# Six instead of four pairs of k's of a down projection as seven products for eight, on one core

## The chip, the cores and the metric

The kernel runs on one core of one Trainium2 chip. The metric is the device time of one execution in microseconds (us): the median of the runs before is 2079.3 us, over three runs from 2079.28 to 2080.11. All matrix work is done in pieces of float32: each operand is split into a high part (`hi`, rounded to the type `float32r`) and the rest (`lo`), and a product is three matmuls: hi x hi, hi x lo and lo x hi.

## The reference

The reference is a block of two layers on an activation `h` of 256 rows and 2048 columns. The first layer mixes with an S5 scan and a gated recurrence, the second with sliding-window attention. After each there is the same feed-forward part, and the change lies in its last product:

```python
def squared_relu_mlp(xn, w_up, w_down):
    return jnp.square(jax.nn.relu(xn @ w_up)) @ w_down

h = h + y.astype(h.dtype)
h = h + squared_relu_mlp(rms_norm(h, mlp_norm[layer]), mlp_w_up[layer], mlp_w_down[layer]).astype(h.dtype)
```

`w_up` is 2048 x 8192 and `w_down` 8192 x 2048, in float32. Every weight is read from HBM once or, in the mixed products below, partly twice.

## The kernel before

**Units.** All weights come in units of 512 KB (128 partitions x 1024 float32), in one list that is written out ahead of the program (`units`). For each unit there is a DMA on the queue of SP (`emit_dma`, line 108 for the units of sums, line 113 for plain ones), a copy on ScalarE (ACT) to the high part (line 141) and a subtraction on VectorE (DVE) to the low part (line 142). `advance` hands the next unit's halves to TensorE (PE) and issues as many DMAs and splits ahead as the buffers allow. Raw units have four buffers of their own (`raw`); while a feed-forward part runs, every odd unit lies instead in one of four "home" buffers in a scratch tile, which the trace calls `chi`. The split halves have four buffers (`whi`, `wlo`) and, for every second odd unit, two more in a scratch tile that the trace calls `clo`.

**The feed-forward part.** The 8192 inner columns are worked off in four chunks of 2048. `up(c)` computes a chunk in eight blocks of 256 columns (32 units); at the end of each block DVE and ACT square, scale and split the result into `ch[c]`. `down(c)` adds the chunk's product with `w_down` to `h`. For the last chunk this is a plain product; for the first three chunks of each layer, six in all, it is `down_mixed`.

**The mixed down projection.** The chunk has 16 k's (blocks of 128 rows of `w_down`), taken as eight pairs. For the columns 0 to 1023 (n = 0 and 1) a pair of k's, the two halves of the 256 rows and the two column halves form a 2 x 2 by 2 x 2 block product. That takes eight products plainly (24 matmuls of 512 columns); the first `NS` = 4 pairs take seven (21 matmuls), from sums of the activations (`forms`, computed at the end of blocks 0 to `NS` - 1 of `up`, lines 1025 to 1032) and from sums of weights (`combine`, line 120 on DVE). A pair's weights come as four units of kinds of their own: "t1" and "t42" in a first half of the stage, "b2" and "b12" (half a unit) in a second. t42 is combined with the raw t1, which has to stay until then, and b12 with the raw b2. On PE a t1, t42 or b2 is 6 matmuls, a b12 3, and a plain unit 12. The columns n = 2 and 3 are plain (16 units) and are strewn between the others; the pairs from `NS` on of n = 0 and 1 are plain units at the end.

**What sets the order.** `down_plan` is the order of the units on PE. The program is scheduled as a whole when it is built, so the order on each engine can differ a little from the order in the code. DVE, ACT and SP work their instructions off in the order that stands there. Scratch tiles such as the block results `r`, the sums `s_` and the copies in `down_mixed` come from one pool of six 4 KB buffers (`t4`).

Of the kernel before, what the change touches and what calls it, by code (L numbers as in the profile page):

```python
# [9 lines left out]
F32R = mybir.dt.float32r  # L10
# [7 lines left out]
P = 128  # L18
# [42 lines left out]
def hybrid_kernel(ctx: ExitStack, tc: tile.TileContext, x, even_norm, even_w_in, s5_lambda_re, s5_lambda_im,  # L61
# [10 lines left out]
    sp = ctx.enter_context(tc.tile_pool(name="sp", bufs=6))  # L72
# [105 lines left out]
    def pump(budget):  # L178
        while side and budget > 0:
            try:  # L180
                budget -= next(side[0])
            except StopIteration:
                side.pop(0)

    def drain(g=None):
        while side and (g is None or g in side):
            pump(1.0)

    def mm(o, a, b, start, stop, **kw):
        PE.matmul(o, a, b, start=start, stop=stop, skip_group_check=True, **kw)  # L190
# [18 lines left out]
    def ublock(XT, kts):  # L209

        acc = psA.tile([P, 2, 2, T], F32, tag="acc", name="acc")
        n = len(kts)
        for i in range(0, n, 4):
            hi, lo = advance()
            for kk in range(4):
                k = kts[i + kk]
                for m in range(2):
                    mm(acc[:, m], hi[:, kk, m * P:(m + 1) * P], XT.both[:, :, k, :], i + kk == 0, False)
                for m in range(2):
                    mm(acc[:, m, 0], lo[:, kk, m * P:(m + 1) * P], XT.hi[:, k, :], False, i + kk == n - 1)  # L220
            pump(SIDE)
        return acc
# [26 lines left out]
    def pm(shape, dtype=F32):  # L249
        return psM.tile(shape, dtype, tag="m", name="m")  # L250

    def t4(shape, dtype=F32):
        return sp.tile(shape, dtype, tag="t4", name="t4")

    def new_pair(kind, shape=(P, KD, T)):
        if kind == "x":
            b = bp.tile([P, 2] + list(shape[1:]), F32R, tag="x", name="x", bufs=1)
            pair = Pair(b[:, 0], b[:, 1])
            pair.both = b
            return pair  # L260
        bufs = 2
        return Pair(bp.tile(list(shape), F32R, tag=kind + "hi", name=kind + "hi", bufs=bufs),
                    bp.tile(list(shape), F32R, tag=kind + "lo", name=kind + "lo", bufs=bufs))
# [43 lines left out]
        ends.append(len(units))  # L307


    NS = 4  # L310
    plain = [(None, n, i) for n in (2, 3) for i in range(8)]
    down_plan = []
    for j in range(NS):
        down_plan += [("t1", 0, j), plain.pop(0), ("t42", 0, j), plain.pop(0)]
        if j < 2:
            down_plan.append(plain.pop(0))
    for j in range(NS):
        down_plan += [("b2", 0, j), plain.pop(0), ("b12", 0, j)]
        if plain and j < 2:
            down_plan.append(plain.pop(0))  # L320
    down_plan += plain + [(None, n, i) for n in (0, 1) for i in range(NS, 8)]

    add_mlp(0)
# [563 lines left out]
    for i in range(10):  # L887
# [14 lines left out]
        hh, j = divmod(i - 2, 4)  # L902
# [81 lines left out]
    def mlp(norm, nxt):  # L984
        XT = norm.XT
        ch, forms = {}, {}
# [20 lines left out]
        def up(c):  # L1007
            ch[c] = new_pair("c")
            if c < 3:
                forms[c] = sp.tile([P, 2, NS, 4, P], F32R, tag="q1", name="forms", bufs=1)  # L1010
            for n in range(8):
                acc = ublock(XT, K16)
                drain()
                r = t4([P, 2, T])
                S.copy(out=r, in_=acc[:, :, 1])
                V.tensor_tensor(out=r, in0=acc[:, :, 0], in1=r, op=ALU.add)
                V.scalar_tensor_tensor(out=r, in0=r, scalar=0.0, in1=rst.unsqueeze(1).to_broadcast([P, 2, T]),
                                       op0=ALU.max, op1=ALU.mult)
                S.activation(out=r, in_=r, func=AF.Square)
                ks = slice(2 * n, 2 * n + 2)  # L1020
                S.copy(out=ch[c].hi[:, ks, :], in_=r)
                V.tensor_tensor(out=ch[c].lo[:, ks, :], in0=r, in1=ch[c].hi[:, ks, :].bitcast(F32),
                                op=ALU.subtract)
                if c < 3 and n < NS:
                    a11, a21, a12, a22 = [r[:, k, t * P:(t + 1) * P] for k in range(2) for t in range(2)]
                    s_ = t4([P, 4, P])
                    for o, a, b, op in ((0, a21, a22, ALU.add), (1, a11, s_[:, 0], ALU.subtract),
                                        (2, a11, a21, ALU.subtract), (3, a12, s_[:, 1], ALU.add)):
                        V.tensor_tensor(out=s_[:, o], in0=a, in1=b, op=op)
                    fh, fl = forms[c][:, 0, n], forms[c][:, 1, n]  # L1030
                    S.copy(out=fh, in_=s_)
                    V.tensor_tensor(out=fl, in0=s_, in1=fh.bitcast(F32), op=ALU.subtract)

        def hadd(t, n, o):
            cs = slice(n * 512, (n + 1) * 512)
            V.tensor_tensor(out=h[:, t, cs], in0=o, in1=h[:, t, cs], op=ALU.add)  # L1036

        def down_mixed(c):
            X, F = ch[c], forms[c]
            a_, c_, e_, f_ = [pm([P, 512]) for _ in range(4)]  # L1040
            half = {0: (a_, f_), 1: (c_, e_)}
            s15, s6v = t4([P, 2, 512]), t4([P, 2, 512])
            s1, s5, s6, v = s15[:, 0], s15[:, 1], s6v[:, 0], s6v[:, 1]
            accs = {}

            def triple(o, fh, fl, wh, wl, start, stop):
                mm(o, fh, wh, start, False)
                mm(o, fh, wl, False, False)
                mm(o, fl, wh, False, stop)

            def whole(k, t):
                return X.hi[:, k, t * P:(t + 1) * P], X.lo[:, k, t * P:(t + 1) * P]

            def form(j, i):
                return F[:, 0, j, i], F[:, 1, j, i]

            for kind, n, j in down_plan:
                hi, lo = advance()
                w = [(hi[:, b], lo[:, b]) for b in range(2)]
                if kind == "t1":  # L1060
                    triple(a_, *whole(2 * j, 0), *w[0], j == 0, False)
                    triple(c_, *form(j, 0), *w[1], j == 0, False)
                elif kind == "t42":
                    triple(f_, *whole(2 * j + 1, 1), *w[0], j == 0, False)
                    triple(e_, *form(j, 1), *w[1], j == 0, False)
                    if j == NS - 1:
                        S.copy(out=s1, in_=a_)
                        S.copy(out=s5, in_=c_)
                        S.copy(out=s6, in_=e_)
                elif kind == "b2":  # L1070
                    triple(a_, *whole(2 * j + 1, 0), *w[0], False, False)
                    triple(c_, *form(j, 3), *w[1], False, False)
                elif kind == "b12":
                    triple(e_, *form(j, 2), *w[0], False, j == NS - 1)
                    if j == NS - 1:
                        V.tensor_tensor(out=v, in0=e_, in1=s1, op=ALU.add)
                        hadd(0, 1, s1)
                        hadd(0, 1, s6)
                        hadd(1, 0, v)
                        hadd(1, 1, v)  # L1080
                        hadd(1, 1, s5)
                else:
                    if n not in accs:
                        if n > 1:
                            acc = psA.tile([P, 2, 512], F32, tag="acc", name="acc")
                            accs[n] = [acc[:, t] for t in range(2)]
                        else:
                            accs[n] = half[n]
                    for t in range(2):
                        for kk in range(2):  # L1090
                            first = j + kk == 0 if n > 1 else n == 1 and t == 1 and j == NS and kk == 0
                            triple(accs[n][t], *whole(2 * j + kk, t), *w[kk], first, j == 7 and kk == 1)
                    if j == 7:
                        for t in range(2):
                            hadd(t, n, accs[n][t])
                    pump(SIDE)
# [12 lines left out]
        for c in range(4):  # L1109
            up(c)  # L1110
            down(c)
# [205 lines left out]
```

## Time and profile before

| | |
|---|---|
| median of the runs | 2079.3 us |
| the profiled execution | 2076.72 us |
| its span, first to last instruction | 2074.9 us |
| PE busy | 2062.2 us |
| DVE busy | 1476.6 us |
| ACT busy | 1137.5 us |
| granted TensorE clock | 1.000 over the span |

"Busy" counts the time in which an engine works on at least one instruction. The durations of matmuls overlap (a matmul of 512 columns is listed with about 390 ns), so the time of one in a stream is read from the distance of two starts. The first mixed down projection lies from 510.73 to 596.39 us.

### The profile page before, as it was taken

To read this page: it belongs to the slowest core of one execution; us is meant where nothing else is said; L and a number is where in the kernel's file an instruction comes from. 1 tells how busy PE (TensorE), PEld (TensorE's weight loads), DVE (VectorE), ACT (ScalarE), POOL (GpSimd) and SP (SyncE) were. 2 spreads that over 40 slices of the span, in tenths; PEclk is the share of its full clock that TensorE was granted. 3 is DMA by queue.
4 is the path that set the end of the run, shared out by engine and by line. 5 is a ranking of instruction groups with operands and counts; after the bars stand their busy time and mean duration, and the time that the engine had idled before them with its cause. 6 is when DMAs were issued, how large, how long until landed. Compare 5 with 4: busy or idle time off the path is not lost. (4 is left out here: it accounts for less than half of the span.)

```text
span 2074.9 us, 31132 instructions
## 1 busy us (share of the span) xinstructions
PE 2062.2 (99%) x12144; PEld 1755.4 (85%) x12144; DVE 1476.6 (71%) x2100; ACT 1137.5 (55%) x1541; POOL 38.8 (2%) x38
## 2 busy tenths in 40 slices
PE   9999999999999999999999999999999999999999
PEld 8988988888888878888888888788888888888887
DVE  6799967777767767776655688777767776776653
ACT  5887554565545545554554477565545545554542
POOL 2000000000000000000000110000000000000000
PEclk9999999999999999999999999999999999999999
DMA  8444557565676586576554643556676576567552
GB/s 250 122 150 145 169 165 245 173 199 193 204 244 191 192 254 190 196 250 197 192 184 125 190 150 125 183 182 203 204 249 188 192 260 192 187 210 247 188 200 89
DMA packets 264739, 397.75 MB, mean 192 GB/s; under 512 B 14888, under 2 KB 148560, under 8 KB 264272
## 3 DMA queue, kind: packets, MB, share of 16 engines
q1 hardware_dynamic: 263168, 392.50, 59.7%
q8 instruction: 95, 1.56, 0.3%
q0 software_dynamic: 672, 2.15, 0.3%
q10 hardware_dynamic: 752, 1.12, 0.2%
q14 instruction: 52, 0.43, 0.1%
HBM read 393.62 MB, written 2.10 MB: 191 GB/s over the span
## 5 line engine op out<-in xcount | busy, mean ns | idle before, releaser
L141 ACT CAST whi<-raw 128x1024 fp32r<-128x1024 f32 (+1 forms) x479 | 494.1, 1034 | 524.8 <-PE acc L190 427.5
L142 DVE TENSOR_TENSOR wlo<-raw,whi 128x1024 fp32r<-128x1024 f32 (+1 forms) x479 | 571.0, 1200 | 243.5 <-ACT whi L141 242.7
L190 PE MATMUL acc<-x,whi 128*128 128x512 f32 (+1 forms) x2336 | 636.0, 359 | 0.0
L190 PEld LDWEIGHTS acc<-x,wlo 128*128 128x128 f32 x1952 | 367.7, 189 | 70.2 <-DVE wlo L142 0.3
L190 PE MATMUL acc<-x,wlo 128*128 128x256 f32 x1952 | 417.9, 279 | 0.1
L190 PEld LDWEIGHTS acc<-x,whi 128*128 128x128 f32 x2336 | 359.6, 190 | 1.5 <-issue 0.4
L190 PE MATMUL acc<-wlo,chi 128*128 128x512 f32 x664 | 260.1, 392 | 2.6 <-DVE wlo L142 2.4
L190 PE MATMUL acc<-whi,chi 128*128 128x512 f32 x664 | 260.4, 392 | 0.0
L190 PE MATMUL acc<-whi,clo 128*128 128x512 f32 x664 | 259.4, 391 | 0.0
L142 DVE TENSOR_TENSOR wlo<-chi,whi 128x1024 fp32r<-128x1024 f32 x138 | 165.5, 1199 | 108.4 <-ACT whi L141 108.3
L141 ACT CAST whi<-chi 128x1024 fp32r<-128x1024 f32 x138 | 142.5, 1032 | 160.7 <-PE acc L190 123.7
L141 ACT CAST clo<-chi 128x1024 fp32r<-128x1024 f32 x136 | 143.0, 1053 | 137.6 <-PE acc L190 110.0
L142 DVE TENSOR_TENSOR clo<-chi,clo 128x1024 fp32r<-128x1024 f32 x136 | 166.1, 1223 | 58.1 <-ACT clo L141 57.0
L190 PE MATMUL acc<-whi,x 128*128 128x512 f32 x576 | 181.4, 393 | 0.0
L190 PE MATMUL acc<-x,clo 128*128 128x512 f32 x960 | 176.9, 337 | 0.0
L190 PEld LDWEIGHTS acc<-x,clo 128*128 128x128 f32 x960 | 150.2, 188 | 21.3
L190 PEld LDWEIGHTS acc<-wlo,chi 128*128 128x128 f32 x664 | 124.7, 188 | 31.7 <-DVE wlo L142 6.8
L190 PEld LDWEIGHTS acc<-whi,chi 128*128 128x128 f32 x664 | 124.7, 188 | 26.4 <-issue 0.8
L190 PEld LDWEIGHTS acc<-whi,clo 128*128 128x128 f32 x664 | 124.7, 188 | 25.3
L190 PEld LDWEIGHTS acc<-whi,x 128*128 128x128 f32 x576 | 107.4, 188 | 22.4 <-issue 0.4
L190 PE MATMUL acc<-clo,chi 128*128 128x512 f32 x400 | 123.1, 389 | 0.0
L120 DVE TENSOR_TENSOR raw<-raw 128x512 f32<-128x512 f32 (+1 forms) x72 | 59.4, 824 | 89.0 <-DMA raw<-in_mlp_w_down_dram 52.7
(260 smaller groups left out, 2399.6 us busy)
## 6 DMA issues: line engine op xcount, KB each, us to landing
chi<-in_mlp_w_down_dram SPq DMA_DIRECT2D x146, 512.0 KB, 3.8
raw<-in_mlp_w_up_dram SPq DMA_DIRECT2D x134, 512.0 KB, 3.8
raw<-in_mlp_w_down_dram SPq DMA_DIRECT2D x134, 512.0 KB, 4.6
chi<-in_mlp_w_up_dram SPq DMA_DIRECT2D x122, 512.0 KB, 3.8
raw<-in_even_w_in_dram SPq DMA_DIRECT2D x79, 512.0 KB, 3.9
raw<-in_odd_w_qkv_dram SPq DMA_DIRECT2D x40, 512.0 KB, 3.7
raw<-in_even_w_out_dram SPq DMA_DIRECT2D x32, 512.0 KB, 4.1
raw<-in_odd_w_out_dram SPq DMA_DIRECT2D x32, 512.0 KB, 3.8
```

What stands on the lines that cost most here:

```text
L120: V.tensor_tensor(out=o, in0=a, in1=b, op=ALU.subtract)
L141: S.copy(out=hi[:, ks], in_=raw[:, ks])
L142: V.tensor_tensor(out=lo[:, ks], in0=raw[:, ks], in1=hi[:, ks].bitcast(F32), op=ALU.subtract)
L190: PE.matmul(o, a, b, start=start, stop=stop, skip_group_check=True, **kw)
```

## The change

`NS` goes from 4 to 6, so that six of the eight pairs of each mixed down projection take seven products. The plan of the units is written anew: in the first half each pair is t1, plain, t42, plain; in the second half the pairs 0, 1, 3 and 4 are b2, plain, b12, and the pairs 2 and 5 are b2, b12; four plain units remain at the end. The tile `forms` still holds four pairs' sums; those of pairs 4 and 5 are put in two of the six scratch buffers of `t4`, and stay there until the last b12.

```diff
-    NS = 4
+    NS = 6
     plain = [(None, n, i) for n in (2, 3) for i in range(8)]
     down_plan = []
     for j in range(NS):
         down_plan += [("t1", 0, j), plain.pop(0), ("t42", 0, j), plain.pop(0)]
-        if j < 2:
-            down_plan.append(plain.pop(0))
     for j in range(NS):
-        down_plan += [("b2", 0, j), plain.pop(0), ("b12", 0, j)]
-        if plain and j < 2:
-            down_plan.append(plain.pop(0))
+        down_plan += [("b2", 0, j)] + ([plain.pop(0)] if j % 3 < 2 else []) + [("b12", 0, j)]
     down_plan += plain + [(None, n, i) for n in (0, 1) for i in range(NS, 8)]
...
             if c < 3:
-                forms[c] = sp.tile([P, 2, NS, 4, P], F32R, tag="q1", name="forms", bufs=1)
+                forms[c] = sp.tile([P, 2, 4, 4, P], F32R, tag="q1", name="forms", bufs=1)
+                forms[c] = [forms[c][:, :, j] for j in range(4)]
...
-                    fh, fl = forms[c][:, 0, n], forms[c][:, 1, n]
+                    if n >= 4:
+                        forms[c].append(t4([P, 2, 4, P], F32R))
+                    fh, fl = forms[c][n][:, 0], forms[c][n][:, 1]
...
             def form(j, i):
-                return F[:, 0, j, i], F[:, 1, j, i]
+                return F[j][:, 0, i], F[j][:, 1, i]
```

On DVE, in the first half of the first mixed down projection, this stands before the change. L120 is a combination, L142 a split; `raw_5673` is t42 of pair 3, `raw_5614` and `raw_5641` are t42 of pair 2 and t1 of pair 3, `raw_5698` and `raw_5738` are the first b2 and b12, and `chi_4782` is the tile of all home buffers.

```order
L142 TENSOR_TENSOR clo_4783<-chi_4782,clo_4783 128x1024
L120 TENSOR_TENSOR raw_5673<-raw_5673 128x512
L120 TENSOR_TENSOR raw_5673<-raw_5641,raw_5673 128x1024
L142 TENSOR_TENSOR wlo_5688<-chi_4782,whi_5687 128x1024
L142 TENSOR_TENSOR wlo_5703<-raw_5614,whi_5702 128x1024
L142 TENSOR_TENSOR wlo_5723<-raw_5641,whi_5722 128x1024
L120 TENSOR_TENSOR raw_5738<-raw_5698,raw_5738 128x512
L142 TENSOR_TENSOR clo_4783<-chi_4782,clo_4783 128x1024
```

After the change a round of the first half reads so on DVE; `raw_5632` and `raw_5657` are t1 and t42 of pair 3, `raw_5691` and `raw_5716` those of pair 4, `raw_5750` and `raw_5775` those of pair 5.

```order
L142 TENSOR_TENSOR wlo_5720<-raw_5632,whi_5719 128x1024
L142 TENSOR_TENSOR wlo_5735<-raw_5657,whi_5734 128x1024
L142 TENSOR_TENSOR clo_4783<-chi_4782,clo_4783 128x1024
L120 TENSOR_TENSOR raw_5750<-raw_5750 128x512
L142 TENSOR_TENSOR wlo_5759<-chi_4782,whi_5758 128x1024
L120 TENSOR_TENSOR raw_5775<-raw_5775 128x512
L120 TENSOR_TENSOR raw_5775<-raw_5750,raw_5775 128x1024
L142 TENSOR_TENSOR wlo_5779<-raw_5691,whi_5778 128x1024
L142 TENSOR_TENSOR wlo_5794<-raw_5716,whi_5793 128x1024
```

The combination of t1 of pair 5 now stands two splits behind the split of t1 of pair 3, whose buffer it takes, and every round of the six has this form.

The second half on DVE after the change, from the first b2 on: `raw_5809` is b2 of pair 0, `raw_5836` its b12, `raw_5896` b2 of pair 2, `raw_5928` and `raw_5956` b2 and b12 of pair 3; `wlo_5940` is the low part of b2 of pair 1, which lies in a home buffer.

```order
L142 TENSOR_TENSOR wlo_5880<-chi_4782,whi_5879 128x1024
L142 TENSOR_TENSOR wlo_5899<-raw_5809,whi_5898 128x1024
L1035 TENSOR_TENSOR h_4035<-t4_5595,h_4035 128x512
L120 TENSOR_TENSOR chi_4782<-raw_5896,chi_4782 128x512
L142 TENSOR_TENSOR wlo_5913<-raw_5836,whi_5912 128x512
L142 TENSOR_TENSOR clo_4783<-chi_4782,clo_4783 128x512
L1035 TENSOR_TENSOR h_4035<-t4_5596,h_4035 128x512
L120 TENSOR_TENSOR raw_5956<-raw_5928,raw_5956 128x512
L142 TENSOR_TENSOR wlo_5940<-chi_4782,whi_5939 128x1024
```

The split of b2 of pair 1 stands behind the combinations of the b12 of pairs 2 and 3, of which the second takes the buffer that the split of b12 of pair 0 frees.

The DMAs on SP for these, after the change; rows of 512 columns are b12, `raw_5871` is a plain unit, and the first two rows in `chi_4782` are b12 and b2 of pair 1.

```order
L108 DMA raw_5836<-in_mlp_w_down_dram 128x512
L108 DMA chi_4782<-in_mlp_w_down_dram 128x512
L108 DMA chi_4782<-in_mlp_w_down_dram 128x1024
L113 DMA raw_5871<-in_mlp_w_down_dram 128x2x512
L108 DMA raw_5896<-in_mlp_w_down_dram 128x1024
L113 DMA chi_4782<-in_mlp_w_down_dram 128x2x512
L108 DMA chi_4782<-in_mlp_w_down_dram 128x512
L108 DMA raw_5928<-in_mlp_w_down_dram 128x1024
L108 DMA raw_5956<-in_mlp_w_down_dram 128x512
```

Before the change b2 and b12 of the first three pairs all lay in the `raw` buffers; now they take `raw` and home buffers in turn, and SP issues them in this order, each when its buffer is free.

## Rows read from the trace of the kernel before

**Rows 1.** The page: the span, and section 1 (busy us, share, instructions).
```profile
span 2074.9 us, 31132 instructions
PE 2062.2 (99%) x12144; PEld 1755.4 (85%) x12144; DVE 1476.6 (71%) x2100; ACT 1137.5 (55%) x1541; POOL 38.8 (2%) x38
```

**Rows 2.** Waits, whole span: who waited for whom, us in total, times, longest.
```profile
ACT whi L141 <- PE acc L190: 551.2, 358, 4.4
...
DVE raw L120 <- DMA raw<-in_mlp_w_down_dram: 52.7, 30, 3.2
DVE raw L120 <- issue: 35.6, 12, 3.8
...
PEld acc L190 <- DVE wlo L142: 7.1, 13, 1.8
```

**Rows 3.** Waits of PE's matmuls alone, whole span.
```profile
PE acc L190 <- DVE wlo L142: 2.4, 3, 1.3
```

**Rows 4.** Timeline of PE: start, duration, line, out<-in, shapes, count, idle before.
```profile
510.73 0.40 PE L190 MATMUL m<-whi,chi 128*128 128x512 f32 x1
...
516.18 0.39 PE L190 MATMUL acc<-whi,chi 128*128 128x512 f32 x1
...
518.90 0.39 PE L190 MATMUL acc<-whi,chi 128*128 128x512 f32 x1
...
558.76 0.50 PE L190 MATMUL acc<-wlo,chi 128*128 128x512 f32 x1 [0.63 <-DVE wlo L142]
...
596.39 0.62 PE L190 MATMUL acc<-x,whi 128*128 128x512 f32 x2
```

**Rows 5.** Timeline of DVE in the first mixed down projection.
```profile
500.64 1.22 DVE L142 TENSOR_TENSOR wlo<-raw,whi 128x1024 fp32r<-128x1024 f32 x1 [1.56 <-ACT whi L141]
...
518.47 0.69 DVE L120 TENSOR_TENSOR raw<-raw 128x512 f32<-128x512 f32 x1 [3.12 <-DMA raw<-in_mlp_w_down_dram]
...
523.69 2.35 DVE L142 TENSOR_TENSOR wlo<-raw,whi 128x1024 fp32r<-128x1024 f32 x2
...
529.52 1.95 DVE L120 TENSOR_TENSOR raw<-raw 128x512 f32<-128x512 f32 x2 [2.34 <-DMA raw<-in_mlp_w_down_dram]
...
537.63 0.69 DVE L120 TENSOR_TENSOR raw<-raw 128x512 f32<-128x512 f32 x1 [2.75 <-issue]
538.24 1.22 DVE L142 TENSOR_TENSOR clo<-chi,clo 128x1024 fp32r<-128x1024 f32 x1
539.37 1.22 DVE L142 TENSOR_TENSOR wlo<-chi,whi 128x1024 fp32r<-128x1024 f32 x1
...
546.72 0.69 DVE L120 TENSOR_TENSOR raw<-raw 128x512 f32<-128x512 f32 x1 [2.66 <-DMA raw<-in_mlp_w_down_dram]
...
555.74 0.69 DVE L120 TENSOR_TENSOR raw<-raw 128x512 f32<-128x512 f32 x1 [3.11 <-issue]
```

**Rows 6.** Timeline of SP's DMA queue in the same stretch.
```profile
513.04 2.07 SPq L108 DMA_DIRECT2D raw<-in_mlp_w_down_dram  x2
...
524.94 1.48 SPq L108 DMA_DIRECT2D raw<-in_mlp_w_down_dram  x2
...
533.76 1.48 SPq L108 DMA_DIRECT2D raw<-in_mlp_w_down_dram  x2
...
541.75 1.48 SPq L108 DMA_DIRECT2D raw<-in_mlp_w_down_dram  x2
...
550.92 0.33 SPq L108 DMA_DIRECT2D raw<-in_mlp_w_down_dram  x1
```

**Rows 7.** Groups of DVE instructions, shapes apart, whole span: busy, mean ns, idle before.
```profile
L1032 DVE TENSOR_TENSOR forms<-t,forms 128x512 fp32r<-128x512 f32 x24 | 16.4, 685 | 0.0
```

**Rows 8.** The page, DMA issues: count, KB each, median us to landing.
```profile
raw<-in_mlp_w_down_dram SPq DMA_DIRECT2D x134, 512.0 KB, 4.6
```

**Rows 9.** The tile `raw` from 495 to 575 us, its last row.
```profile
DMA to landing us min/median/max: 3.1/5.0/9.5
```

**Rows 10.** Timeline of ACT at the start of the stage.
```profile
510.70 1.05 ACT L141 CAST whi<-raw 128x1024 fp32r<-128x1024 f32 x1 [1.73 <-PE acc L190]
```

## The prediction

> **What bounds the kernel now.** I read the page first: TensorE (PE) is busy for 2062.2 of 2074.9 us [rows 1], so 12.7 us of the span is all that it ever loses, and only fewer matmuls, or a new loss, can move the time by much. The table of waits says who paces whom: the copies of the weights on ACT wait most of all for PE (551.2 us), that is, they run as far ahead as their buffers allow and then stand; the subtractions that build the sums of weights (line 120, on DVE) wait for transfers, 52.7 us put down to DMA and 35.6 us to "issue" [rows 2]. PE itself waits for DVE's splits for 7.1 us on its weight-load row [rows 2] and 2.4 us on its matmul row [rows 3]; these overlap. So the stock of ready weights is thin only where sums are built, in the six mixed down projections.
>
> The first of these starts on PE at 510.73 and ends with the next up projection at 596.39: 85.66 us. Twelve matmuls of one unit take 516.18 to 518.90, which is 0.2267 us each; the one long stop is before 558.76 [rows 4]. Before the change the stage has 372 such matmuls (4 pairs x 21, 16 units of 12 for the columns n = 2, 3, and 8 units of 12), 84.33 us, so 1.3 us is loss.
>
> DVE is a queue in order. A combination pitches at 0.6 us, a split of 1024 at 1.135 us (537.63, 538.24, 539.37), and five times it stands 2.3 to 3.1 us for a transfer before line 120 [rows 5]. From the issue on SP to the end of that stand: 524.94 to 529.52 is 4.58 us, 513.04 to 518.47 is 5.43, 533.76 to 537.63 is 3.87, 541.75 to 546.72 is 4.97, 550.92 to 555.74 is 4.82 [rows 5, 6]. Each issue comes right behind a split that frees its buffer: 523.69 with 2.35 us for two splits puts the first one's end at 524.9 [rows 5], and SP issues at 524.94 [rows 6]. So there is a circle: split, buffer free, transfer, combine, split. Before the change it turns about as fast as PE works: 524.94, 533.76, 541.75, 550.92 [rows 6] are 8.8, 8.0 and 9.2 us apart.
>
> **The change part by part.** *Matmuls removed.* Two pairs more, 3 matmuls each, in six stages: 36 x 0.2267 = 8.2 us less, 1.36 us per stage, all on the path. 366 matmuls make 82.97 us.
>
> *Work added.* Each of the two pairs has 3.5 units of weights in place of 2, three combinations of 512 and one of 1024, and in the up projection four short subtractions, a copy and a subtraction for its form (0.685 us for the last [rows 7]). In the up projection I cost that at nothing: ACT there still waits for PE, and PE's unit is longer than what DVE does in it; were that cover gone, it would be about 1.4 us per form (that row and four subtractions of a quarter of its columns), 12 forms, 17 us at most. Two of the six scratch buffers are held; a block needs two or three at a time and PE takes four units for one block, so I cost this at nothing too.
>
> *What moves: the circle.* Six rounds of t1, plain, t42, plain now follow each other without the fifth unit that the first two rounds had. PE needs 1.36 + 2.72 + 1.36 + 2.72 = 8.16 us for a round (6, 12, 6 and 12 matmuls). All t1 and t42 lie in the four `raw` buffers, all plain units in the home buffers. By the order, the split of t1 of pair j frees the buffer for t1 of pair j+2, and that transfer is awaited two splits later. From one t1 split's end to the next: transfer, combination 0.6, a plain split 1.135, combinations 0.6 and 1.135, split 1.135; that is the transfer plus 4.6 us. For the transfer I take 4.6 us, the row at 524.94 (the most alike: a whole unit, behind plain ones) and also the page's median [rows 8]; the tile's own median is 5.0 [rows 9]. A round is then 9.2 us, and DVE loses 1.0 us on PE in each.
>
> The stock lasts as follows. The t1 split of pair 0 ends where the row at 500.64 does, near 501.8 [rows 5], 8.9 us ahead of PE. Pair 1's cannot be earlier than ACT's copy, which waits for PE until 510.70 [rows 10], and follows a transfer and two splits: 513.15. Pair 2's round has two more operations of the up block and one more plain split, 6.35 instead of 4.6: 524.1. Then 533.3, 542.5, and for pair 5 (it waits for the first b12, issued at 543.65, lands 4.8 later, and has two additions of 0.6 before it) 551.4. PE wants them at 510.7 + 8.16 j, for pair 5 at 551.5. So the t half just passes, with its stock spent.
>
> The b half has less matmul time for each transfer: b2, b12 without a plain unit between them is 2.04 us. Its chain on DVE: combination of b12 (1), then three splits, to 555.4; that frees the home buffer for b12 of pair 2, awaited for 4.8 us (the row at 550.92, half a unit behind whole ones): combined at 560.8. Split of b12 (0): 561.4; that frees the buffer for b12 (3), 3.9 us (the shortest row, at 533.76, since here the issue before it is 5 us old): combined at 565.9. Only then, in DVE's queue, comes the split of b2 (1): 567.05. PE comes to it at 551.5 + 8.16 + 1.36 + 2.72 + 0.68 and needs its low part 0.23 later, 564.7: a stop of 2.35 us. This split frees the buffer of b2 (4): 4.6 us, combination, plain split, split of b12 (2) at 574.0, wanted at 573.2 (0.8); b2 (3) at 575.15, wanted at 574.7 (0.45); its b12 (5) 4.8 us, combination, two splits, b2 (4) at 581.15, wanted at 579.9 (1.2). Together 4.8 us of stops, and a stage of 87.8 us.
>
> *The sum.* Six stages: -8.2 + 6 x 4.8 = +20.6 us, less what the stages lose now. That is between 2.4 and 7.1 us [rows 2, 3]; the first stage alone has 1.3, I take 5. Net +15.6 us on the profiled execution's 2076.7 (2074.9 of span and 1.8 around it), 2092.3. The median of the runs, 2079.3, lies 2.6 above that execution: 2095.
>
> *Bounds of the transfer.* With 3.9 us for every one a t round takes 8.5 us, the stock lasts to the b half, and about 0.3 us of stops is left: 6 x 0.3 - 8.2 - 5 = -11 us, 2068. With 5.4 us for every one the t half runs dry too: 3.5 us there and 8.7 in the b half by the same steps, +59 us, 2138. With 4.5 it is 4.0 us per stage, +11 us. A tenth of a microsecond of landing time is worth about 6 us.
>
> The Trainium skill (DMA: Bandwidth & Descriptors, Anatomy of one DMA) has a fixed 2.0 us and 436 bytes per nanosecond for one transfer, from POOL's queue: an estimate of 3.2 us for a unit of 512 KB, by which the circle would be faster than PE and the change worth its full gain. The trace disagrees for these transfers on SP's queue: 4.58 us from issue to use [rows 5, 6]; I go by the row.
>
> **The rivals.** *The transfers land soon enough (faster).* If they take 3.9 us, as one of five did, the matmuls saved remain and part of today's stops goes: 2068. For it: DVE and ACT have room, and with t units and plain units in different buffers every other one, the b half shares eight buffers more evenly than now. Against: four of the five stands took longer, and the stage asks for more bytes in less time (20.5 MB in 83.0 us, before 19 in 84.3, units of 512 KB and halves counted from the plan). It decides at about 4.2 us.
>
> *No difference.* At about 4.2 us the stops (2.2 us per stage) eat what is saved: 2079.
>
> *Worse than forecast.* The denser transfers slow each other to 5.0 us and above: 2105 or more. For it: the medians of 5.0 [rows 9] and the stand of 5.43; against: today's rows hold such crowding already.
>
> *The matmuls don't go.* The order shows the plan's new sequence, seven products for pairs 4 and 5; this I leave out of the sum.
>
> **How the numbers follow.** The forecast's case, slower by 5 to 35 us, has 0.65, of which 0.15 is the worse one; its own range is 2084 to 2114. Transfers soon enough: 0.23. No difference within 0.2% (4.2 us, about what can be told here): 0.12. For eight in ten I go from the first rival's 2069 to 2114.
>
> **What would show it.** Right: PE stops of 1 to 3 us in each of the six stages at the splits of b2 (1), b12 (2) and b2 (4), each with DVE standing for a transfer just before; t1 issues on SP about 9 us apart; a stage of 86 to 90 us; the matmul pitch still 0.227. Wrong: stages near 83 us; the issue-to-use time under 4.2 us; or stops in the up projection, which would be the forms or the scratch buffers.

## The result, and the profile after

The changed kernel takes 2097.03 us (median of four runs, 2093.57 to 2098.71); the kernel before, run beside it, takes 2079.44 us. The ratio is 1.0087, with an interval from 1.0074 to 1.01: slower by 17.6 us, where 2095 us had been forecast. The profiled execution took 2098.71 us.

The page of the changed kernel answers to [rows 1]: span, then busy time, share and instructions of each engine.

```profile
span 2096.6 us, 31288 instructions
PE 2064.7 (98%) x12108; PEld 1753.0 (84%) x12108; DVE 1547.6 (74%) x2232; ACT 1161.9 (55%) x1577; POOL 38.8 (2%) x38
```

The 36 matmuls are gone (12144 to 12108), so the rival by which they don't go falls. But PE is busy 2.5 us longer than before, and the span has grown by 21.7 us. PE now idles 31.9 us where it idled 12.7. By the matmuls saved its busy time should have fallen by 8.2 us. Of the difference, 6.4 us are matmuls at a lower clock, which come below; most of the rest comes with the stops: at each, the whole listed 0.39 us of a matmul counts, of which a stream shows 0.227, and the matmul after it takes 0.336.

The table of waits, whole span (who waited for whom, us in total, times, longest), answers to [rows 2, 3].

```profile
DVE raw L120 <- DMA raw<-in_mlp_w_down_dram: 85.8, 67, 2.7
DVE chi L120 <- DMA chi<-in_mlp_w_down_dram: 49.2, 21, 4.4
PEld m L190 <- DVE wlo L142: 29.3, 24, 2.9
...
PE m L190 <- DVE wlo L142: 20.2, 16, 2.5
```

PE's matmuls waited for DVE's splits for 2.4 us before and wait 20.2 now; DVE's combinations (line 120) stand for transfers 135 us. (Below, a *stand* is DVE or GpSimd waiting for a transfer, and a *stop* is PE waiting.) The home buffers (named `chi` here, after the array whose memory they use) are among them with 49.2 us: units of sums lie in them as well, and their transfers too come after they are wanted.

The next view cuts the trace at the six mixed stages, from the first matmul of each to the first of the up projection behind it: window, length, PE busy (matmuls that overlap it, two or three more than begin in it), granted clock, DMA share, GB/s. First the kernel before, then the changed one.

```profile
510.73:596.39 85.66, 85.00 (x375) 1.00 0.72 237
...
sum 511.30, PE 508.73; mean PE 84.79
```

```profile
511.92:601.10 89.18, 84.81 (x369) 1.00 0.71 236
690.26:780.07 89.81, 84.87 (x368) 1.00 0.71 235
869.24:957.08 87.84, 84.95 (x368) 0.98 0.72 238
1472.63:1560.66 88.03, 85.21 (x368) 0.98 0.73 240
1649.82:1738.25 88.43, 85.17 (x369) 0.98 0.72 241
1827.41:1915.91 88.50, 85.39 (x368) 0.98 0.72 240
sum 531.79, PE 510.40; mean PE 85.07
```

The stages hold 20.5 of the 21.7 us. Each lasts 87.8 to 89.8 us where its matmuls make 82.97. The GB/s are those of before, although the stage asks for more; that this is no limit of the transfers is seen in a run below, where 260 GB/s arrive in the same stages.

Now the stop that is alike in all six. The timeline of PE of the changed kernel (start, duration, line, out<-in, shapes, count, idle before) at b2 of pair 1:

```profile
566.96 0.39 PE L190 MATMUL m<-whi,chi 128*128 128x512 f32 x1
569.48 0.50 PE L190 MATMUL m<-wlo,chi 128*128 128x512 f32 x1 [2.13 <-DVE wlo L142]
```

The matmul with the high part runs; the one with the low part comes 2.52 us later instead of 0.23. DVE's queue in that stretch shows why:

```profile
558.13 1.22 DVE L142 TENSOR_TENSOR wlo<-raw,whi 128x1024 fp32r<-128x1024 f32 x1
...
563.69 0.69 DVE L120 TENSOR_TENSOR chi<-raw,chi 128x512 f32<-128x512 f32 x1 [3.74 <-DMA chi<-in_mlp_w_down_dram]
564.30 0.69 DVE L142 TENSOR_TENSOR wlo<-raw,whi 128x512 fp32r<-128x512 f32 x1
...
567.60 0.69 DVE L120 TENSOR_TENSOR raw<-raw 128x512 f32<-128x512 f32 x1 [1.41 <-DMA raw<-in_mlp_w_down_dram]
568.21 1.22 DVE L142 TENSOR_TENSOR wlo<-chi,whi 128x1024 fp32r<-128x1024 f32 x1
```

The split that PE wants is the last row; it ends at 569.43. Its own weights had landed by 554.11, when a combination read them, and their high part was ready at 561.21. Ahead of it in the queue stand two combinations of later units, each waiting for its transfer (3.74 and 1.41 us). SP's queue has the issues of those two:

```profile
558.24 0.33 SPq L108 DMA_DIRECT2D chi<-in_mlp_w_down_dram  x1
559.37 5.97 SPq L108 DMA_DIRECT2D raw<-in_mlp_w_down_dram  x2
```

From 558.24 to 563.69 the first took 5.45 us. The second of the pair begins at the end of the 5.97 us, near 565.0, right behind the split of 564.30, and is used at 567.60, 2.6 us later. Are the DMA engines full meanwhile? The windows view has the two stands, the stretch behind them, and a stretch of the third stage (columns busy time of PE, PEld, DVE, ACT, POOL, then clock, DMA share, GB/s):

```profile
559.90:563.70 3.80, 3.80 (x18) 3.14 (x17) 0.06 (x2) 2.37 (x3) 0.00 (x0) 1.00 0.86 311
566.20:567.60 1.40, 1.15 (x6) 0.61 (x4) 0.00 (x0) 1.12 (x2) 0.00 (x0) 1.00 0.82 297
567.30:569.30 2.00, 0.05 (x1) 0.00 (x0) 1.70 (x2) 0.75 (x2) 0.00 (x0) 1.00 0.16 58
...
926.60:929.30 2.70, 2.70 (x6) 2.14 (x7) 2.21 (x2) 0.17 (x1) 0.00 (x0) 0.50 0.64 167
```

While DVE stands, the DMA engines are busy 86% and 82% of the time, against 71% over the stage; most of PE's stop, with 16%, lies behind that, while DVE does the second combination and then the split. So transfers that are asked for late (each right behind the split that frees its buffer) and a crowd of them come together in the stands, and this view doesn't part the two. The runs below do: with the same bytes, PE stops or doesn't by what stands behind the wait. And behind the stop of the third stage the granted clock is 0.50, the lower level of 1.2 GHz, for 2.7 us:

```profile
923.68 0.39 PE L190 MATMUL m<-whi,chi 128*128 128x512 f32 x1
926.60 0.79 PE L190 MATMUL m<-wlo,chi 128*128 128x512 f32 x1 [2.53 <-DVE wlo L142]
...
928.04 0.63 PE L190 MATMUL m<-wlo,forms 128*128 128x512 f32 x1
928.47 0.63 PE L190 MATMUL m<-whi,forms 128*128 128x512 f32 x1
```

There the matmuls are 0.427 us apart instead of 0.227.

### The profile page after: what moved, and what is told of

Same layout as the page of the kernel before. It is cut to its first block, busy times and chain, and to the rows that moved or that the text cites. A ratio compares the mean times of both kernels' runs of the same rounds, so it can differ in the third digit from the quotient of the medians.

```text
span 2096.6 us, 31288 instructions
## 1 busy us (share of the span) xinstructions
PE 2064.7 (98%) x12108; PEld 1753.0 (84%) x12108; DVE 1547.6 (74%) x2232; ACT 1161.9 (55%) x1577; POOL 38.8 (2%) x38
## 4 chain that ended last, share of the span: by engine, by line
PE 77%; DMA 10%; DVE 8%; issue 3%; ACT 1%; SPq 0%; DVEq 0%; ACTq 0%
PE acc L190 65%; PE m L190 10%; DMA raw<-in_mlp_w_down_dram 6%; DVE wlo L142 5%; DMA chi<-in_mlp_w_down_dram 4%; DVE clo L142 1%; DVE raw L120 1%; PE m L382 1%; PE m L1209 1%; ACT chi L656 0%; DMA xt<-in_x_dram 0%; ACT whi L141 0%; DVE t L675 0%; DMA chi<-in_mlp_w_up_dram 0%; PE m L478 0%
## 5 line engine op out<-in xcount | busy, mean ns | idle before, releaser
L142 DVE TENSOR_TENSOR wlo<-raw,whi 128x1024 fp32r<-128x1024 f32 (+1 forms) x491 | 587.7, 1205 | 210.7 <-ACT whi L141 209.8
L190 PE MATMUL acc<-whi,chi 128*128 128x512 f32 x616 | 242.7, 394 | 0.0
L190 PE MATMUL acc<-whi,clo 128*128 128x512 f32 x616 | 240.7, 391 | 0.0
L190 PE MATMUL acc<-wlo,chi 128*128 128x512 f32 x616 | 240.7, 391 | 0.0
L142 DVE TENSOR_TENSOR wlo<-chi,whi 128x1024 fp32r<-128x1024 f32 (+1 forms) x144 | 169.4, 1176 | 78.7 <-ACT whi L141 78.6
L141 ACT CAST clo<-chi 128x1024 fp32r<-128x1024 f32 (+1 forms) x142 | 144.1, 1016 | 150.1 <-PE acc L190 122.4
L141 ACT CAST whi<-chi 128x1024 fp32r<-128x1024 f32 (+1 forms) x144 | 146.1, 1015 | 125.5 <-PE acc L190 99.1
L142 DVE TENSOR_TENSOR clo<-chi,clo 128x1024 fp32r<-128x1024 f32 (+1 forms) x142 | 166.7, 1175 | 42.1 <-ACT clo L141 35.5
L120 DVE TENSOR_TENSOR raw<-raw 128x512 f32<-128x512 f32 (+1 forms) x120 | 102.1, 851 | 86.9 <-DMA raw<-in_mlp_w_down_dram 85.8
L190 PE MATMUL acc<-clo,chi 128*128 128x512 f32 x496 | 153.8, 389 | 0.0
```

The costliest lines, as they stand in the source:

```text
L120: V.tensor_tensor(out=o, in0=a, in1=b, op=ALU.subtract)
L141: S.copy(out=hi[:, ks], in_=raw[:, ks])
L142: V.tensor_tensor(out=lo[:, ks], in0=raw[:, ks], in1=hi[:, ks].bitcast(F32), op=ALU.subtract)
```

## The experiments

The theory: the loss is the circle in DVE's queue, above all a combination of a later unit that waits for its transfer ahead of a split that PE wants now. Its rivals: the forms and the held scratch buffers cost the time; the bytes or the landing times do; every pair costs the same. The kernel before took 2079.6 us in the runs beside all of these (25 and 10 executions).

**Forms and scratch alone.** The kernel before with its plan of four pairs, plus the work of six forms, two of them in scratch tiles that stay held. Pairs 2 and 3 use the sums of pairs 4 and 5, and their own are left unused.

```diff
-                forms[c] = sp.tile([P, 2, NS, 4, P], F32R, tag="q1", name="forms", bufs=1)
+                forms[c] = sp.tile([P, 2, 4, 4, P], F32R, tag="q1", name="forms", bufs=1)
+                forms[c] = [forms[c][:, :, j] for j in (0, 1)] + [None, None] + [forms[c][:, :, j] for j in (2, 3)]
...
-                if c < 3 and n < NS:
+                if c < 3 and n < 6:
...
+                    m_ = (0, 1, 4, 5, 2, 3)[n]
+                    if m_ in (2, 3):
+                        forms[c][m_] = t4([P, 2, 4, P], F32R)
```

> The kernel before with only the side work of the change: the forms of six pairs are computed in each up projection (two of them are used by nothing), and the forms of pairs 2 and 3 lie in two of the six scratch buffers until the last b12. The plan of the units stays that of four pairs. Theory (the loss lies in DVE's queue order: splits that PE needs stand behind a combination that waits for a transfer): the forms and the held buffers cost nothing, 2079 us, within 3. Rival (the added vector work or the two missing scratch buffers slow the up projections): a good part of the 18 us lost, 2086 to 2097, with PE's stops in the up projections.

It took 2078.28 us, ratio 0.9995 (0.9984 to 1.0006). What the prediction cost at nothing costs nothing.

**Five pairs.** The changed kernel with five pairs, each with a plain unit in the second half.

```diff
-    NS = 6
+    NS = 5
...
-        down_plan += [("b2", 0, j)] + ([plain.pop(0)] if j % 3 < 2 else []) + [("b12", 0, j)]
+        down_plan += [("b2", 0, j), plain.pop(0), ("b12", 0, j)]
```

> Five pairs instead of six, and in the second half each pair has a plain unit between b2 and b12. 18 matmuls fewer than the kernel before, 4.1 us. Theory: in this order only one combination with a late transfer (that of b12 of pair 2) stands ahead of the split of b2 of pair 1 where six pairs have two, and no pair is bare; about 1 us of stops per stage instead of 5.5, so 2076 us (2072 to 2082), and the clock at 1.00. Rival (the loss goes with the bytes or the vector work added, pair by pair): half of what six pairs lose, about 2088.

It took 2085.72 us, ratio 1.0024 (1.0013 to 1.0035): the theory's number was missed, and the rival's (about 2088) is the nearer one. The stages tell more (columns as in the views of the six stages):

```profile
510.43:594.94 84.51, 84.00 (x371) 1.00 0.77 249
684.11:774.69 90.58, 86.54 (x371) 0.98 0.72 234
863.85:948.20 84.35, 83.95 (x372) 1.00 0.77 252
...
1815.07:1905.60 90.53, 85.74 (x372) 1.00 0.74 238
```

Three stages, every second one, are as the theory wants them (0.7 us over their 369 matmuls, 83.65); the three between lose 5 to 7 us. Five pairs make 42 units a stage; four and six make 40 and 44. The rule for the two extra split buffers goes by the unit's number modulo four (`home(i) and i % 4 == 1`), so with 42 units other units get them in every second stage. That was a guess at this point; a run below tests it.

**Order of one combination.** The changed kernel; the combination of each b12 may only be queued on DVE behind the split of the unit before it, so that no earlier split stands behind it.

```diff
+            if kind == "b12":
+                with tc.issue_after(last_lo[0].ins):
+                    V.tensor_tensor(out=o, in0=a, in1=b, op=ALU.subtract)
+            else:
+                V.tensor_tensor(out=o, in0=a, in1=b, op=ALU.subtract)
```

> The changed kernel (six pairs, the same units, bytes and arithmetic) with one rule more for DVE's queue: the combination of a b12 is issued only behind the split of the unit ahead of it in the plan, so that the split of b2 of pair 1 stands ahead of the combinations of the b12 of pairs 2 and 3. Theory: the stop of 2.1 to 2.7 us at b2 of pair 1 goes in all six stages, and with it the fall of the clock behind it in four; the stops of about 1 us in the first half stay, smaller ones at later b12 may come. 2078 us (2072 to 2086). Rival (the transfers as such are too slow for what the stage asks): the stop only moves to the next unit, 2093 to 2099.

It took 2074.45 us, ratio 0.9976 (0.9966 to 0.9987): the loss is gone, and the kernel is faster than before. At b2 of pair 1 PE now runs through, here in the first stage (the added lines make line 190 into 195):

```profile
567.51 0.39 PE L195 MATMUL m<-whi,chi 128*128 128x512 f32 x1
567.74 0.39 PE L195 MATMUL m<-wlo,chi 128*128 128x512 f32 x1
```

The clock is 1.00 in all six stages, whose sum is 510.5 us. What remains are stops of 1.0 to 1.7 us in the first half of the stages, 12.3 us with the small ones, at splits of t1. Nothing in the matmuls, the bytes or the buffers was changed: the order alone held the 21 us that the stages had more.

**Combinations on GpSimd.** The changed kernel with line 120 on GpSimd (POOL), so that a combination stands in a queue in which no split waits.

```diff
-            V.tensor_tensor(out=o, in0=a, in1=b, op=ALU.subtract)
+            G.tensor_tensor(out=o, in0=a, in1=b, op=ALU.subtract)
```

> The changed kernel with all combinations (line 120) on GpSimd instead of DVE, so that DVE's queue never waits for a transfer of its own accord. Theory: the stops of the first half go as well as those of the second, 2066 to 2074 us, if GpSimd needs no more than about 1.5 us for a combination of 512 and 3 us for one of 1024 (8.16 us of PE per round hold three of 512, or two and one of 1024). If its rows show twice that, GpSimd is the new bound: 2100 and above. Rival (bytes or DMA bandwidth): unchanged, 2093 to 2099, whatever GpSimd's rows.

It took 2063.04 us (2062.76 to 2063.32), ratio 0.9915 (0.9893 to 0.9936): below the theory's range, although GpSimd needs more than the theory allowed it (1.82 us in the mean for most combinations of 512, 3.15 for one of 1024). Its first stage, from the first row to the second in the timeline of PE:

```profile
510.64 0.40 PE L190 MATMUL m<-whi,chi 128*128 128x512 f32 x1
...
593.61 0.61 PE L190 MATMUL acc<-x,whi 128*128 128x512 f32 x2
```

That is 82.97 us, the sum of 366 matmuls, and all six stages are the same to 0.01 us. The transfers are no sooner there (medians of 4.3 us to landing, where the changed kernel has 4.4 and 4.0), and somebody still waits for them:

```profile
POOL raw L120 <- DMA raw<-in_mlp_w_down_dram: 95.9, 43, 6.8
POOL chi L120 <- DMA chi<-in_mlp_w_down_dram: 84.9, 20, 8.1
```

181 us of standing, up to 8.1 us at a time, and PE doesn't stop in any of these stages, in which 259 to 262 GB/s arrive (235 to 241 in the changed kernel). So neither the landing time nor the bytes set the changed kernel's time, but who stands behind the one that waits.

**The control: four pairs with GpSimd.** The same line moved in the kernel before.

> The kernel before, four pairs a stage, with nothing changed but the engine of the combinations of raw blocks (line 120): GpSimd instead of VectorE. Theory (the gain of the six-pair kernel with this move is the matmuls that six pairs save, once nothing stands behind a combination's wait): this kernel keeps its 372 matmuls a stage, loses only its own stops (about 5 us in six stages), every mixed stage becomes 372 x 0.2267 = 84.33 us, and it takes about 2074 us (2072 to 2077). Rival (the move to GpSimd by itself is the gain, and six pairs bring nothing): 2063 to 2066 us, as the six-pair kernel with it.

It took 2072.33 us, ratio 0.9963 (0.995 to 0.9976); each stage is 84.33 us, without a stop. The move alone brings 7 us and leaves each stage at its 372 matmuls. The other 9.3 us between this kernel and the one with six pairs are the matmuls saved (8.2, the change's own gain) and 1.1 more. In the profiled executions a difference of this kind lies ahead of the first mixed stage: PE begins it at 512.43 us here and at 510.64 there, and here it waited 2.19 us for the transfer of `x` at the start of the kernel, there not. That lies ahead of all that the pairs touch.

**Five pairs, the rule shifted.** The five-pair kernel; the number in the rule for the split buffers is shifted by two at the end of every mixed stage.

```diff
+    def turn(i):
+        return i + 2 * sum(b <= i for b in turns)
...
-        if home(i) and i % 4 == 1:
+        if home(i) and turn(i) % 4 == 1:
...
+            turns.append(len(units))
```

> Five pairs as before (42 transfers a stage), but the rule that says which transfers are split into the two scratch buffers is shifted by two at the end of every mixed stage, so that each stage meets it as its first one does. Theory (the three slow stages of the first run with five pairs, 88.7 to 90.6 us, are slow since 42 is not a multiple of four, and the split buffers fall to other blocks there): all six stages take 84.3 to 84.6 us, and the time is 2073 to 2077 us. Rival (the loss belongs to five pairs, each stage's own chance of falling late, whatever buffers the blocks get): three or so stages stay at 88 to 91 us, and the time stays at 2083 to 2088 us.

It took 2071.76 us, ratio 0.9958 (0.9942 to 0.9975), a little under what the theory gave. In its profiled execution (2075.26 us):

```profile
511.88:597.77 85.89, 84.43 (x371) 1.00 0.77 247
...
1462.60:1546.25 83.65, 83.65 (x371) 1.00 0.78 252
...
sum 508.81, PE 503.95; mean PE 83.99
```

No stage is over 86 us: the slow ones came from the buffer rule. Not all is as expected (84.3 to 84.6 in each): three lose 1.8 to 2.2 us, one 1.0 and two nothing. The first stage, where the rule is the same in both runs, lost 0.9 in the first run and 2.2 here, so a difference of about 1 us in one stage of one execution is not read here. The loss is not one per pair. That it goes by which buffer a unit gets, and so by when that buffer is freed and which transfer is late, is argued.

**Seven pairs with GpSimd.** Can the better kernel go on? Beside `NS` and the plan, this run has line 120 on GpSimd and the shifted rule of the run before.

```diff
-            V.tensor_tensor(out=o, in0=a, in1=b, op=ALU.subtract)
+            G.tensor_tensor(out=o, in0=a, in1=b, op=ALU.subtract)
...
-    NS = 6
+    NS = 7
...
-        down_plan += [("b2", 0, j)] + ([plain.pop(0)] if j % 3 < 2 else []) + [("b12", 0, j)]
+        down_plan += [("b2", 0, j)] + ([plain.pop(0)] if plain and j % 3 == 1 else []) + [("b12", 0, j)]
```

> Seven pairs a stage with the combinations on GpSimd (46 transfers a stage, three sums held in scratch, the rule of the split buffers shifted by two a stage). Theory (only matmuls count as long as no stop comes): 363 matmuls a stage, 82.29 us, six stages 4.1 us less than with six pairs: 2059 us (2057 to 2062). Rival (the transfers run out: in the second half of the pairs 9 matmuls, 2.04 us, take 768 KB, and only two plain blocks are left to lie between): PE stops there for transfers in every stage, 2 to 4 us each, and the time is 2068 to 2080 us.

It took 2072.76 us, ratio 0.9966 (0.9954 to 0.9978), the rival's number but not its place: PE's stops, 14.8 us in the six stages, are mostly in the first half, and they are for DVE's splits. They are 10.7 us more than the 4.1 us of matmuls saved, and the span is 10.7 us longer than with six pairs. PE in the second stage, then GpSimd, then DVE (the added lines make 120, 142 and 190 into 126, 148 and 196; GpSimd's row takes in one combination of 1024):

```profile
723.53 0.39 PE L196 MATMUL acc<-whi,chi 128*128 128x512 f32 x1
725.07 0.50 PE L196 MATMUL acc<-wlo,chi 128*128 128x512 f32 x1 [1.15 <-DVE wlo L148]
```

```profile
713.85 10.09 POOL L126 TENSOR_TENSOR raw<-raw 128x512 f32<-128x512 f32 x4
```

```profile
711.57 3.41 DVE L148 TENSOR_TENSOR wlo<-chi,whi 128x1024 fp32r<-128x1024 f32 x1
714.90 4.54 DVE L148 TENSOR_TENSOR wlo<-raw,whi 128x1024 fp32r<-128x1024 f32 x2
719.36 3.41 DVE L148 TENSOR_TENSOR clo<-chi,clo 128x1024 fp32r<-128x1024 f32 x1
722.70 2.32 DVE L148 TENSOR_TENSOR wlo<-chi,whi 128x1024 fp32r<-128x1024 f32 x1
```

A split that takes 1.22 us alone takes 2.3 to 3.4 us beside GpSimd's combinations, so five of them need 13.4 us in this stretch, without a gap, and PE's stop ends with the last. Six pairs on GpSimd is the best of the kernels run: 0.85% faster than the kernel before.

## Why the prediction came out right

**The mechanism.** (As in the prediction, the t half is the first half of a stage, with t1 and t42, the b half the second, and b2 (1) is b2 of pair 1.) The forecast's circle holds: the transfers into the buffers that the splits of t1 free, t1 (3), t1 (4), t1 (5) and then b2 (0), are issued in the first stage at 516.06, 526.93, 536.55 and 545.93, 10.9, 9.6 and 9.4 us apart, where about 9 had been given and PE takes 8.16. The stop at b2 (1), behind two standing combinations, had been worked out as 2.35 us; it is 2.29, 2.60, 2.69, 2.06, 2.63 and 2.47 in the six stages. Moving the standing combination behind the split took that stop away in all six, and taking the combinations out of DVE's queue took all stops away. The two transfers behind it were, in the first stage, 5.45 and 2.6 us from issue to use, where 4.8 and 3.9 had been taken: 8.05 against 8.7, the errors cancel in part.

**The sizes.** From starts of matmuls over the six stages, stops per stage:

| term | forecast | measured, mean of six |
|---|---|---|
| b2 (1) | 2.35 | 2.5 |
| stops in the t half | 0 | 1.4 |
| later stops of the b half, with small ones | 2.45 | 0.5 |
| slow matmuls at the lower clock | 0 | 1.1 |
| together | 4.8 | 5.5 |

The stages are in fact 5.7 us longer than their matmuls; the last 0.2 is spread over gaps too small to list. The total is near, but two terms are wrong one way and one the other, so it is closer than the working deserved: that is luck.

*The t half.* "The t half just passes, with its stock spent" failed. Two things were mis-sized. Its rounds had one transfer in the circle; the timeline of DVE shows two stands a round, the second for t42, issued 1.1 us behind t1:

```profile
530.44 0.69 DVE L120 TENSOR_TENSOR raw<-raw 128x512 f32<-128x512 f32 x1 [1.26 <-DMA raw<-in_mlp_w_down_dram]
...
533.43 1.95 DVE L120 TENSOR_TENSOR raw<-raw 128x512 f32<-128x512 f32 x2 [1.17 <-DMA raw<-in_mlp_w_down_dram]
...
544.68 2.35 DVE L142 TENSOR_TENSOR wlo<-raw,whi 128x1024 fp32r<-128x1024 f32 x2
```

The transfer of t1 (4) itself was shorter (526.93 to 530.44, 3.5 us against 4.6), so the round is 9.6 and not 9.2. And the stock was thinner: the split of t1 (1) ended near 516.0, not 513.15 (a time for which the prediction shows no working), while the stage began only 1.2 us later. So the split of t1 (4) ended at 545.9, a little over 1 us after PE wanted it.

*The later stops.* b12 (2), b2 (3) and b2 (4) had 2.45 us; the first two stages show stops in that stretch (2.3 and 0.9 us; in the first it begins at b12 (4)), the other four none. In those four the slow matmuls behind b2 (1) give DVE 1.4 to 1.7 us to catch up; that this is what covers the stops is argued from the timeline, not tested.

*The clock.* "The matmul pitch still 0.227" was wrong for seven to nine matmuls in each of four stages, 6.4 us of the 20.5. The prediction had put the clock at nothing, by the pitch of before.

**The rivals.** "The transfers land soon enough" was decided by the wrong quantity. The median to landing did fall (4.4 and 4.0 against 4.6 [rows 8]), and six pairs became slower all the same. Two of the three t1 transfers above, 3.5 and 3.2 us from issue to use, even lie under the 4.2 at which the prediction saw the decision and a sign of being wrong: what it has right is the circle and the stop, not that bound. What decides is how many stands lie in the queue ahead of a wanted split. The sentence "a tenth of a microsecond of landing time is worth about 6 us" holds at most in that one order of DVE's queue, which a scheduler may change; the prediction's own bounds (-11 us at 3.9, +15.6 at 4.6, +59 at 5.4) make it 4 to 5.5. "Worse than forecast" and "no difference" did not come. The forms and the scratch buffers, costed at nothing, cost nothing (0.9995).

**The sum.** The stops of before, taken as 5 us, are 4.9 by the starts of its matmuls. Six stages of 87.8 had been forecast, 526.6 us, and 531.8 came; another 1.2 lies outside the stages. The profiled execution is thus 6.4 us over the forecast for it, 2092.3. The 2.6 us added for the median had the wrong sign, since the profiled execution of the changed kernel was its slowest (1.7 above its median): 6.4 - 2.6 - 1.7 leaves the 2.1 us between 2095 and 2097.

## What to carry to other kernels

When work that waits for a transfer shares an in-order queue with work that the bounding engine wants, price each stand by what is queued behind it, not by the engine's busy share: VectorE was busy 74% of the time here and cost 20 us, and was busier (78%) and harmless once the waiting instructions had left its queue. A saving of a few matmuls that speeds up the turn of the buffers can then cost more than it saves, and the order of one kind of instruction, or moving it to a nearly idle engine, gives the gain back. Look as well at rules that go by a unit's number: 42 units instead of 40 put every second stage into another pattern.

## What the runs showed of the hardware

**The clock after a stop.** After stops of 2.69, 2.06, 2.63 and 2.47 us PE ran its next matmuls 0.427 us apart, at a granted clock of 0.50, until the pitch was back at 0.227; after the stops of 2.29 and 2.60 us in the first two stages it did not, nor after any stop of before, the longest 1.5 us. In the five-pair kernel it did after a stop of 2.76 us and not after one of 2.04. So here a stop of 2 to 3 us could cost 1.4 to 1.7 us more than its length, and not always; what tells the cases apart these runs don't show. The Trainium skill (TensorE: Matmul & The Clock Gate, Part 1: The HAM clock gate) gives 426.7 ns from start to start for 512 columns at the lower level, and the trace agrees.

**VectorE beside GpSimd.** With the combinations on GpSimd, DVE's splits take longer (each group of instructions with its count, then busy us and mean ns; six pairs):

```profile
L142 DVE TENSOR_TENSOR wlo<-raw,whi 128x1024 fp32r<-128x1024 f32 x477 | 646.9, 1362 | 220.6 <-ACT whi L141 218.9
L142 DVE TENSOR_TENSOR wlo<-chi,whi 128x1024 fp32r<-128x1024 f32 x132 | 212.4, 1609 | 89.6 <-ACT whi L141 89.0
...
L120 POOL TENSOR_TENSOR raw<-raw 128x512 f32<-128x512 f32 x84 | 153.0, 1824 | 580.3 <-DVE t L1026 372.5 <-DMA raw<-in_mlp_w_down_dram 95.9 <-DVE clo L1019 83.9
```

The first two are 1220 and 1221 ns in the changed kernel, and a combination of 512 is 691 ns on DVE. The single instructions show how. Of the 739 splits of 1024 columns at six pairs, the 564 that no combination touches take 1.19 to 1.23 us. The 121 that begin while a combination runs end, nearly all of them, 1.08 us after that combination does; the 54 that were running when one began take 1.21 to 1.23. So a split waits until the combination that it meets is over: the splits of 3.41 us above met one of 1024 with 2.3 us to go. The Trainium skill (SBUF — State Buffer, Who interferes with whom) says that a DVE instruction with two inputs in SBUF contends with a GpSimd instruction that reads SBUF, and calls the contention an exclusive lock on the ports that the two share. The trace agrees. At six pairs this stays hidden; at seven it is what delays the splits for which PE stops.
